# A decoder trunk: the gate of the recurrent layer as a stage of its own with seven products, and the last recurrent block in two token halves

## The chip, the cores and the metric

One core of a Trainium2 chip runs one program. The metric is the device time of one execution in microseconds (us). TensorE does the matrix products, VectorE and ScalarE the elementwise work, GpSimd some elementwise work and the loads that add onto what lies in the buffer, SyncE issues the other loads and stores. Each engine runs its instructions in a fixed order and waits on semaphores.

## The reference

Two layers on 16 learned tokens and 1024 frames, width 1024: a latent attention layer, then a gated linear recurrence. What matters here is the second layer and the end:

```python
def rglru_mixer(h, w_in, conv_w, conv_b, w_rg, b_rg, w_ig, b_ig, lam, w_out):
    proj = h @ w_in
    u, gate = jnp.split(proj, [LRU_WIDTH], axis=-1)
    up = jnp.pad(u, ((0, 0), (CONV_WIDTH - 1, 0), (0, 0)))
    uc = conv_b + up[:, 0:T] * conv_w[0]
    for j in range(1, CONV_WIDTH):
        uc = uc + up[:, j:j + T] * conv_w[j]
    ub = uc.reshape(B, T, LRU_BLOCKS, LRU_BLOCK)
    r = jax.nn.sigmoid(jnp.einsum('btgi,gij->btgj', ub, w_rg).reshape(B, T, LRU_WIDTH) + b_rg)
    i = jax.nn.sigmoid(jnp.einsum('btgi,gij->btgj', ub, w_ig).reshape(B, T, LRU_WIDTH) + b_ig)
    log_a = -LRU_C * r.astype(jnp.float32) * jax.nn.softplus(-lam.astype(jnp.float32))
    a = jnp.exp(log_a)
    mult = jnp.sqrt(-jnp.expm1(2.0 * log_a))
    ...
    b = mult * (i * uc).astype(jnp.float32)
    _, hs = lax.associative_scan(combine, (a, b), axis=1)
    y = hs.astype(h.dtype) * jax.nn.silu(gate)
    return y @ w_out
```

Then come the residual add, a last normalisation, and the output of the 1024 frames. Four recurrent blocks of 256 channels make the 1024 channels.

## The kernel before, in words

Channels lie on the partitions, tokens along the rows. A product of two float32 numbers is made of three matmuls on a high and a low part (`mm3`, lines 86 to 88): high by high, low by high, high by low. `hi_of` (line 80, ScalarE) makes a high part, `lo_of` (line 83, VectorE) the low part as the difference. So each operand of TensorE costs one pass of ScalarE and one of VectorE first.

The normalised input of the second layer is `x2h`, `x2l`, made tile by tile of 128 tokens out of the attention layer's output product (`ao`) and transposes (`xt_b`). Then, by column tile `ct` of 128 channels:

- `b_u(ct)`: the recurrent path, `pu` = 72 matmuls of about 348 columns, copied to `up`, and the convolution `uc` (one ScalarE pass, three VectorE taps), split into `uh` and `ul`.
- `b_gate(ct)`: the gate, `pg` = 2 chunks of 24 matmuls of 512 columns; ScalarE takes the sigmoid, VectorE multiplies with the bank: `Y`.
- `b_rec(blk)`: both gates of the recurrence for two column tiles, `pz` = 72 matmuls, a sigmoid for each bank, then exponential and tanh over 1040 tokens, then the root (each group of functions behind a table load), then VectorE's multiplies and the scan over all tokens (line 813).
- `b_mul(ct)`: `Y` times the scan's result, two halves of 512 tokens, on GpSimd (line 822).

The order by block: gates of the block, recurrence, then `b_u` of the next block. So between a block's convolution and its `pz` stand one or two gate tiles. The last gate (`ct` 7) runs behind the last `pz`.

The output product `b` at the end is cut into quarters: tokens in two halves, channels in two halves, columns in two halves, with seven products of 48 matmuls in place of eight, on sums and differences of quarters (`a11`, `a12`, `a21`, `a22` are quarters of `Y` by channel and token half, `y_split` splits them, `ych`/`ycl` and `y1`, `y7` are the parts). The sums of weights are made by loads that add onto the buffer, issued by GpSimd (`wchain`, `wt`).

The framework orders each engine's instructions from its own estimate of time, so the rows of an engine don't stand in the order of the code. `behind` keeps ScalarE's groups of functions together.

## Time and profile before

| | |
|---|---|
| runs | 915.93, 918.11, 918.83 us; median 918.11 |
| profiled execution | 920.09 us, its span 918.30 us |
| TensorE, VectorE, ScalarE, GpSimd busy | 97%, 64%, 51%, 5% of the span |
| loads and stores | 72.25 MB, 79 GB/s mean |

The span is that of the profiled instructions; the rest of the profiled time lies around it. Busy time of TensorE counts each matmul from start to its modelled end, and neighbours overlap.

### The profile page before, as it was taken

The page shows a single profiled execution, that of the slowest core. Times are in us where ns is not written, and L with a number is a line of the kernel's source. Part 1 is how long each engine was busy: PE and PEld are TensorE (multiplying, and loading weights), DVE is VectorE, ACT ScalarE, POOL GpSimd, SP SyncE. Part 2 cuts the span into 40 slices and gives each one's busy share as a digit, 9 for nine tenths or more (in the row PEclk, how much of TensorE's full clock was granted, in tenths as well). Part 3 has the DMA queues.
Part 4 walks back from the last instruction along what each step waited for, and adds up shares of the span by engine and source line. Part 5 has one row for each costly group of instructions (what it writes and reads, how often), then busy time and mean ns, then how long its engine had stood idle before and what let it go on. Part 6 is the DMA issues. An engine that isn't in the chain of part 4 may idle for free.

```text
...
## 1 busy us (share of the span) xinstructions
...
## 2 busy tenths in 40 slices
...
GB/s 273 47 58 92 64 130 129 83 71 57 16 57 16 17 55 17 16 63 16 17 53 98 144 90 159 87 93 46 46 46 46 47 46 47 92 92 229 137 70 183
DMA packets 71169, 72.25 MB, mean 79 GB/s; under 512 B 15056, under 2 KB 52688, under 8 KB 71104
## 3 DMA queue, kind: packets, MB, share of 16 engines
...
## 4 chain that ended last, share of the span: by engine, by line
PE 92%; ACT 3%; DVE 2%; issue 1%; DMA 1%; SPq 0%; ACTq 0%; DVEq 0%
PE pt L536 4%; PE pu L88 3%; PE ga L86 3%; PE pu L86 3%; PE ga L87 3%; PE ga L88 3%; PE pu L87 3%; PE ao L86 3%; PE ao L88 3%; PE ao L87 3%; PE pg L87 3%; PE pg L88 3%; PE pg L86 3%; PE s L491 2%; PE b L86 2%; PE b L88 2%
## 5 line engine op out<-in xcount | busy, mean ns | idle before, releaser
L509 ACT ACTIVATE p<-s,m 116x116 f32<-116x116 f32 (+4 forms) x80 | 55.3, 693 | 42.9 <-PE pt L536 15.2
L80 ACT ACTIVATE pth<-pt 116x348 fp32r<-116x348 f32 (+5 forms) x152 | 57.5, 396 | 29.4 <-PE pt L536 25.8
L83 DVE TENSOR_TENSOR ptl<-pt,pth 116x348 fp32r<-116x348 f32 (+5 forms) x152 | 64.1, 438 | 10.3 <-ACT pth L80 9.8
L88 PE MATMUL pu<-x2h,l_wu 128*128 128x348 f32 (+1 forms) x192 | 61.5, 321 | 0.4 <-DVE l_wu L83 0.4
L86 PE MATMUL ga<-xth,h_wg 128*128 128x348 f32 (+1 forms) x192 | 61.7, 321 | 0.0
L88 PE MATMUL ga<-xth,l_wg 128*128 128x348 f32 (+1 forms) x192 | 61.7, 321 | 0.0
L87 PE MATMUL pu<-x2l,h_wu 128*128 128x348 f32 (+1 forms) x192 | 61.7, 321 | 0.0
L86 PE MATMUL pu<-x2h,h_wu 128*128 128x348 f32 (+1 forms) x192 | 61.7, 322 | 0.0
L87 PE MATMUL ga<-xtl,h_wg 128*128 128x348 f32 (+1 forms) x192 | 61.6, 321 | 0.0
L501 DVE CUSTOM_DVE_ANT_0 s<-s,maskt 116x116 f32<-116x116 f32 (+8 forms) x72 | 49.4, 686 | 17.8 <-PE s L495 17.7
L536 PE MATMUL pt<-ident,p 116*116 116x116 f32 (+1 forms) x360 | 54.6, 263 | 2.3 <-DVE ptl L83 1.8
L86 PE MATMUL ao<-wah,yh_a 128*128 128x512 f32 x128 | 50.5, 396 | 2.1 <-ACT yh_a L80 1.5
L87 PE MATMUL pg<-x2l,h_wbg 128*128 128x512 f32 x128 | 50.6, 395 | 0.0
L88 PE MATMUL ao<-wah,yl_a 128*128 128x512 f32 x128 | 50.3, 395 | 0.0
L88 PE MATMUL pg<-x2h,l_wbg 128*128 128x512 f32 x128 | 50.3, 393 | 0.0
L86 PE MATMUL pg<-x2h,h_wbg 128*128 128x512 f32 x128 | 50.2, 392 | 0.0
L87 PE MATMUL ao<-wal,yh_a 128*128 128x512 f32 x128 | 49.9, 391 | 0.0
L491 PE MATMUL s<-kh,qh 128*116 128x348 f32 (+7 forms) x120 | 42.1, 351 | 6.7 <-ACT p L509 6.7
L536 PEld LDWEIGHTS pt<-ident,p 116*116 116x116 f32 (+1 forms) x360 | 41.4, 135 | 6.0 <-DVE ptl L83 2.5
L87 PE MATMUL o<-ptl,v 116*128 116x348 f32 (+1 forms) x144 | 45.8, 318 | 0.0
L88 PE MATMUL o<-pth,v 116*128 116x348 f32 (+1 forms) x144 | 44.6, 310 | 0.0
L86 PE MATMUL o<-pth,v 116*128 116x348 f32 (+1 forms) x144 | 43.6, 303 | 0.0
...
## 6 DMA issues: line engine op xcount, KB each, us to landing
wg<-in_a_w_in SPq DMA_DIRECT2D x8, 512.0 KB, 4.0
wa<-in_a_w_out SPq DMA_DIRECT2D x8, 512.0 KB, 3.5
wu<-in_b_w_in SPq DMA_DIRECT2D x8, 512.0 KB, 4.2
wbg<-in_b_w_in SPq DMA_DIRECT2D x8, 512.0 KB, 3.9
hr<-hscr SPq DMA_DIRECT2D x8, 512.0 KB, 6.7
...
x<-in_x SPq DMA_DIRECT2D x7, 512.0 KB, 3.3
wq<-in_b_w_out SPq DMA_DIRECT2D x6, 512.0 KB, 3.5
```

What stands on the lines that cost most here:

```text
L80: nc.scalar.activation(dst, src, AF.Copy)
L83: nc.vector.tensor_tensor(dst, src, bc(hi), ALU.subtract)
L86: nc.tensor.matmul(ps, lh, rh, start=start, stop=False, **kw)
L87: nc.tensor.matmul(ps, lh, rl, start=False, stop=False, **kw)
L88: nc.tensor.matmul(ps, ll, rh, start=False, stop=stop, **kw)
L491: nc.tensor.matmul(ps, a, kth[:, k0:k0 + w], start=True, stop=False)
L501: MKD[h, t] = nc.vector.tensor_tensor_reduce(pv, pv, mk, 1.0, -NEG, ALU.add, ALU.min, m[:, s:s + 1])
L509: MK[h, t] = nc.scalar.activation(dst, pv, AF.Exp, bias=mx, scale=-1.0, accum_out=l[:, s:s + 1])
L536: nc.tensor.transpose(pv[:nk, j], p[:, k0:k0 + nk], ident[:n, :n])
```

## The change: what it does

The gate becomes a stage in front of the recurrence, for all 1024 channels and frames. It is cut into quarters as the output product is: seven products `g1`, `g2`, `g7`, `g6`, `g4`, `g5` and one more onto `g5`'s banks, each 4 banks x 4 k x 3 matmuls of 512 columns, on quarters of `x2` or on sums of them (`x_sum`, `x_split`: `sum_s3` and others, over 2048 elements a partition), with weight quarters and sums of them (`gchain`, `gt1`). The results are added up in `Y`, and ScalarE applies one SiLU at the end.

The recurrence then has `pu` of the next block ahead of `pz` of this one, and the convolution of a block behind the recurrence of the block before. The last block runs its exponentials, roots, multiplies and scan in two token halves, its `pz` in four chunks, and VectorE multiplies `Y`. Residual rows of the first half are loaded earlier.

```diff
-    hs_ = {}
-    after = []
-    us = {0: [b_u(0), b_u(1)]}
-    gates = {0: [0], 1: [1, 2], 2: [3, 4], 3: [5, 6]}
...
-    for blk in range(NBLK):
-        for ct in gates[blk]:
-            b_gate(ct)
-            gated.add(ct)
-        settle()
-        b_rec(blk, us.pop(blk))
-        settle()
-        if blk + 1 < NBLK:
-            us[blk + 1] = [b_u(2 * blk + 2), b_u(2 * blk + 3)]
...
+    def gate_product(banks, w, xx, first=True):
+        xh, xl = xx
+        for m in range(4):
+            for k in range(4):
+                mm3(banks[m], w[0][k // 2][:, k % 2, m * P:(m + 1) * P], w[1][k // 2][:, k % 2, m * P:(m + 1) * P],
+                    xh[:, k], xl[:, k], first and k == 0, k == 3, skip_group_check=True)
+
+    def x_sum(name, tag, a, b):
+
+        s_ = pbg.tile([P, 4, 512], F32, name=f"sum_{name}", tag=tag, bufs=1)
+        bs = [bc(b_) for b_ in b] if isinstance(b, tuple) else [b]
+        nc.vector.tensor_tensor(s_, bc(a[0]), bs[0], ALU.subtract)
+        nc.vector.tensor_tensor(s_, s_, bc(a[1]), ALU.add)
+        for b_ in bs[1:]:
+            nc.vector.tensor_tensor(s_, s_, b_, ALU.subtract)
+        return s_
...
+    x11, x12, x21, x22 = xq(0, 0), xq(1, 0), xq(0, 1), xq(1, 1)
...
+    b1 = four("g1")
+    gate_product(b1, w1, x11)
+    r2 = w_raw("gq21")
+    w_load(r2, 1, 0, w=w_gate)
+    w2 = w_split(r2, pw1, "gq21")
+    for m in range(4):
+        nc.scalar.activation(cq(0, 0, m), b1[m], AF.Copy)
+        nc.scalar.activation(cq(0, 1, m), b1[m], AF.Copy, scale=-1.0)
+    b2 = two_two("g2")
+    gate_product(b2, w2, x12)
+    s3 = x_sum("s3", "suma", x21, x11)
+    w7 = w_split(ra, wpg, "gt3")
+    s2 = x_sum("s2", "sumb", x22, s3)
+    y7 = x_split(s3, "s3")
+    w_load(ra, 0, 0, True, w=w_gate)
+    for m in range(4):
+        nc.vector.tensor_tensor(cq(0, 0, m), b2[m], cq(0, 0, m), ALU.add)
+        silu(0, 0, m)
+    b7 = four("g7")
+    gate_product(b7, w7, y7)
+    w6 = w_split(ra, pw1, "gt2")
+    y6 = x_split(s2, "s2")
+    s1 = x_sum("s1", "suma", x11, s2)
+    s4 = x_sum("s4", "sumc", x12, s2)
...
+    b6 = two_two("g6")
+    gate_product(b6, w6, y6)
...
+        for p0, p1 in parts:
+            ex = []
+            for o in range(2):
+                ct = 2 * blk + o
+                r, a = ri[o][0][:, p0:p1], as_[o][:, p0:p1]
+                ex.append(behind(sig, nc.scalar.activation, a, r, AF.Exp, 0.0, c8[:, ct:ct + 1]))
+                ex.append(behind(sig, nc.scalar.activation, r, r, AF.Tanh, 0.0, c4[:, ct:ct + 1]))
+            sig = []
+            for o in range(2):
+                sig.append(behind(ex, nc.scalar.activation, ri[o][0][:, p0:p1], ri[o][0][:, p0:p1], AF.Sqrt))
...
+    us = conv_pair(0, u_pair(0))
+    for blk in range(LASTB):
+        ups = u_pair(blk + 1)
+        if blk + 1 == LASTB:
+            st_x2.close()
+            st_hr, phr = open_pool("hr", bufs=1)
+            hr = [phr.tile([P, D], F32, name=f"hr{i}") for i in range(4)]
+            for i in range(4):
+                nc.sync.dma_start(hr[i], hscr[NMETA + i * P:NMETA + (i + 1) * P, :])
+            st_b3, pb3 = open_pool("b3", bufs=2)
+        b_rec(blk, us)
+        for o in range(2):
+            b_mul(2 * blk + o)
+        if blk + 1 == LASTB:
+            pool_of = lambda ct: pb3
+        us = conv_pair(blk + 1, ups)
+    HALF = NMETA + 512
+    b_rec(LASTB, us, [(c, 264) for c in (0, 264)] + [(c, 256) for c in (528, 784)], ((0, HALF), (HALF, T)))
...
-    y2 = yc(a12, "a12")
...
+    y2 = y_pair("y2", a12, 1, (("z0", "z0"), ("z1", "z1")))
```

How the instructions stand then, at three places. First VectorE of the changed kernel around `suml_s3`, the low half that the third gate product streams (`l_gt2` are low halves of weights, `Y<-g2` the combinations with the banks of the second product, lines 820 to 823 are `x_sum`); before, none of these rows exists.

```order
L820 TENSOR_TENSOR sum_s3_6966<-x2h_6171 128x2048
L83 TENSOR_TENSOR x2l_6172<-xt_b7_1_6770,x2h_6171 128x4x128
L83 TENSOR_TENSOR l_gt3_1_6975<-gchain_1_6837,h_gt3_1_6974 128x1024
L866 TENSOR_TENSOR Y_1217<-g2_0_6914,Y_1217 128x512
L821 TENSOR_TENSOR sum_s3_6966<-sum_s3_6966,x2l_6172 128x2048
L866 TENSOR_TENSOR Y_1217<-g2_1_6915,Y_1217 128x512
L823 TENSOR_TENSOR sum_s3_6966<-sum_s3_6966,x2l_6172 128x2048
L866 TENSOR_TENSOR Y_1217<-g2_2_6916,Y_1217 128x512
L83 TENSOR_TENSOR l_gt2_0_7048<-gchain_0_6836,h_gt2_0_7047 128x1024
L866 TENSOR_TENSOR Y_1217<-g2_3_6917,Y_1217 128x512
L820 TENSOR_TENSOR sum_s2_6978<-x2h_6171,sum_s3_6966 128x2048
L83 TENSOR_TENSOR l_gt2_1_7052<-gchain_1_6837,h_gt2_1_7051 128x1024
```

The row that follows is `suml_s3`; so it stands behind the combination with the last bank of the second product and a pass of the next sum.

Second, VectorE where the convolution of the last block is made (`uc` the taps, `ul` the low halves that its `pz` needs). Before, from block 2's last scan on:

```order
L813 SCALAR_TENSOR_TENSOR z_0_8009<-a_8062,z_1_8034 128x1040
L768 SCALAR_TENSOR_TENSOR uc_8165<-up_8085,cwt,uc_8165 128x1040 x2
L83 TENSOR_TENSOR l_wq_0_8529<-wq_0_8524,h_wq_0_8528 128x1024
L768 SCALAR_TENSOR_TENSOR uc_8165<-up_8085,cwt,uc_8165 128x1040
L83 TENSOR_TENSOR ul_8171<-uc_8165,uh_8170 128x1040
```

And in the changed kernel (`Y<-Y` is the difference of two quarters of `Y`, `y1l` and `y7h` parts of the output product's operands, `z_1` the multiply of block 2's input gate):

```order
L927 SCALAR_TENSOR_TENSOR uc_8506<-up_8273,cwt,uc_8506 128x1040
L1028 TENSOR_TENSOR Y<-Y 128x4x512
L927 SCALAR_TENSOR_TENSOR uc_8497<-up_8187,cwt,uc_8497 128x1040
L927 SCALAR_TENSOR_TENSOR uc_8506<-up_8273,cwt,uc_8506 128x1040
L970 TENSOR_TENSOR z_1_8400<-z_1_8400,uc_8163 128x1040
L927 SCALAR_TENSOR_TENSOR uc_8497<-up_8187,cwt,uc_8497 128x1040
L927 SCALAR_TENSOR_TENSOR uc_8506<-up_8273,cwt,uc_8506 128x1040
L1037 CAST y7h_8715<-Y 128x1024
L1037 CAST y7h_8719<-Y 128x1024
L788 SCALAR_TENSOR_TENSOR y1l_8712<-Y,y1h_8711 128x1024
L83 TENSOR_TENSOR l_wt_0_8786<-wchain_8702,h_wt_0_8785 128x1024
L970 TENSOR_TENSOR z_1_8450<-z_1_8450,uc_8172 128x1040
```

The row after `y7l` that follows these is `ul` of the first tile; so work for the output product now stands between the taps and `ul`, which it did not.

Third, TensorE ahead of the last block's `pz`. Before, a gate tile ends there:

```order
L86 MATMUL pg_1_8362<-x2h,h_wbg_8331 128x512
L87 MATMUL pg_1_8362<-x2l,h_wbg_8331 128x512
L88 MATMUL pg_1_8362<-x2h,l_wbg_8332 128x512
L86 MATMUL pz_0_0_8399<-uh_8170,h_wri_8394 128x348
L87 MATMUL pz_0_0_8399<-ul_8171,h_wri_8394 128x348
```

Now `pz` of the block before ends there, and six matmuls that need `uh` alone stand first:

```order
L88 MATMUL pz_1_2_8467<-uh_8177,l_wri_8372 128x344
L86 MATMUL pz_0_0_8523<-uh_8502,h_wri_8518 128x264
L86 MATMUL pz_0_1_8531<-uh_8502,h_wri_8518 128x264
L86 MATMUL pz_0_2_8539<-uh_8502,h_wri_8518 128x256
L86 MATMUL pz_0_3_8547<-uh_8502,h_wri_8518 128x256
L86 MATMUL pz_1_0_8556<-uh_8502,h_wri_8518 128x264
L86 MATMUL pz_1_1_8564<-uh_8502,h_wri_8518 128x264
L87 MATMUL pz_0_0_8523<-ul_8503,h_wri_8518 128x264
```

The gate tiles between the two are gone, and the first matmul of the block that needs `ul` is the seventh.

## Rows read from the trace of the kernel before

**Rows 1.** Busy time by stretch: us, then each engine's busy us (instructions), clock, DMA.

```profile
606.50:811.70 205.20, 205.13 (x1143) 190.34 (x1144) 127.84 (x125) 109.58 (x148) 24.23 (x22) 1.00 0.23 60
...
823.00:911.50 88.50, 87.84 (x393) 71.83 (x391) 82.67 (x122) 49.71 (x74) 10.65 (x8) 1.00 0.52 146
```

**Rows 2.** Timeline of TensorE: start, duration, line, tiles, pairs of neighbours.

```profile
640.20 0.39 PE L87 MATMUL pg<-x2l,h_wbg 128*128 128x512 f32 x1
640.43 0.39 PE L88 MATMUL pg<-x2h,l_wbg 128*128 128x512 f32 x1
...
755.83 0.32 PE L87 MATMUL pz<-ul,h_wri 128*128 128x348 f32 x1
755.99 0.32 PE L88 MATMUL pz<-uh,l_wri 128*128 128x348 f32 x1
...
909.35 0.28 PE L86 MATMUL b<-h_wt,ych_a 128*128 128x256 f32 x1
909.47 0.28 PE L87 MATMUL b<-l_wt,ych_a 128*128 128x256 f32 x1
```

**Rows 3.** Timeline of VectorE: a scan, two taps, and four neighbours of other sizes.

```profile
779.32 2.32 DVE L813 TENSOR_TENSOR_SCAN z<-a,z 128x1040 f32<-128x1040 f32 x1
...
788.26 2.61 DVE L768 SCALAR_TENSOR_TENSOR uc<-up,cwt,uc 128x1040 f32<-128x1040 f32 x2
...
849.07 0.68 DVE L960 TENSOR_TENSOR hr<-b,hr 128x512 f32<-128x512 f32 x1
849.67 2.28 DVE L1020 TENSOR_TENSOR Y<-Y 128x2048 f32<-128x2048 f32 x1
851.87 1.21 DVE L83 TENSOR_TENSOR l_wq<-wq,h_wq 128x1024 fp32r<-128x1024 f32 x1
853.01 0.68 DVE L962 TENSOR_TENSOR hr<-hr,b 128x512 f32<-128x512 f32 x1
```

**Rows 4.** Timeline of ScalarE: a table load, exponentials, tanh, and two of 512.

```profile
767.21 1.28 ACT L308 ACT_TABLE_LOAD   x1
768.50 2.22 ACT L308 ACTIVATE a<-z,c 128x1040 f32<-128x1040 f32 x2
770.63 2.20 ACT L308 ACTIVATE z<-z,c 128x1040 f32<-128x1040 f32 x2
...
807.70 1.06 ACT L308 ACTIVATE Y<-pg 128x512 f32<-128x512 f32 x2
```

**Rows 5.** Timelines of TensorE and VectorE: where `pu` begins to run, the last `x2l`.

```profile
606.57 0.43 PE L88 MATMUL pu<-x2h,l_wu 128*128 128x348 f32 x1 [0.42 <-DVE l_wu L83]
...
615.82 0.69 DVE L83 TENSOR_TENSOR x2l<-xt_b,x2h 128x512 fp32r<-128x512 f32 x1 [0.23 <-ACT x2h L80]
```

**Rows 6.** DMA issues: the loads that add, KB each, median us to landing.

```profile
wchain<-in_b_w_out POOLq DMA_DIRECT2D x6, 512.0 KB, 6.1
```

**Rows 7.** Timelines of GpSimd and VectorE: multiplies on GpSimd, alone and beside VectorE.

```profile
687.74 1.30 POOL L822 TENSOR_TENSOR Y<-Y,z 128x512 f32<-128x512 f32 x1 [0.46 <-DVE Y L837]
...
781.78 4.37 POOL L822 TENSOR_TENSOR Y<-Y,z 128x512 f32<-128x512 f32 x2 [32.04 <-DVE z L813]
...
784.93 3.41 DVE L813 TENSOR_TENSOR_SCAN z<-a,z 128x1040 f32<-128x1040 f32 x1
```

**Rows 8.** Busy time by stretch, as rows 1, where the granted clock fell.

```profile
506.00:507.00 1.00, 0.97 (x6) 0.89 (x6) 0.57 (x2) 0.66 (x2) 0.00 (x0) 0.70 0.70 246
507.00:508.00 1.00, 1.00 (x6) 1.00 (x5) 0.55 (x2) 0.35 (x2) 0.00 (x0) 0.50 0.05 16
...
509.00:510.00 1.00, 1.00 (x6) 1.00 (x5) 0.00 (x0) 0.00 (x0) 0.00 (x0) 0.59 0.00 0
510.00:511.00 1.00, 1.00 (x8) 1.00 (x7) 0.00 (x0) 0.00 (x0) 0.00 (x0) 1.00 0.91 299
```

**Rows 9.** Timeline of TensorE there: the wait before it, and two neighbours in it.

```profile
504.10 0.93 PE L536 MATMUL pt<-ident,p 116*116 116x116 f32 x5 [1.22 <-DVE ptl L83]
...
508.24 0.49 PE L87 MATMUL o<-ptl,v 116*128 116x344 f32 x1
508.52 0.49 PE L88 MATMUL o<-pth,v 116*128 116x344 f32 x1
```

More of the change, by code (lines that the diff above doesn't have):

```diff
@@ new lines, in x_sum, with x_split @@
+    def x_sum(name, tag, a, b):
[6 more added lines that the diff above has]
+        return s_
+    def x_split(s_, name):
+        xh = pbg.tile([P, 4, 512], F32R, name=f"sumh_{name}", tag="sumh", bufs=2)
+        xl = pbg.tile([P, 4, 512], F32R, name=f"suml_{name}", tag="suml", bufs=2)
+        hi_of(xh, s_)
+        lo_of(xl, s_, xh)
+        return xh, xl
@@ new lines, in four, with two_two, silu @@
+    def four(name):
+        return [ps_m(f"{name}_{m}") for m in range(4)]
+    def two_two(name):
+        return [(ps_m if m < 2 else ps_t)(f"{name}_{m}") for m in range(4)]
+    def silu(tq, nq, m):
+        v = cq(tq, nq, m)
+        nc.scalar.activation(v, v, AF.Silu)
+    x11, x12, x21, x22 = xq(0, 0), xq(1, 0), xq(0, 1), xq(1, 1)
+    r1 = w_raw("gq11")
+    w_load(r1, 0, 0, w=w_gate)
+    w1 = w_split(r1, wpg, "gq11")
+    ra = w_raw("gchain")
+    w_load(ra, 0, 1, w=w_gate)
+    w_load(ra, 1, 1, True, w=w_gate)
@@ new lines, in trunk @@
+    w4 = w_split(ra, wpg, "gt4")
+    r5 = w_raw("gt1")
+    w_load(r5, 0, 0, w=w_gate)
+    w_load(r5, 0, 1, True, w=w_gate)
+    for m in range(4):
+        nc.vector.tensor_tensor(cq(1, 1, m), b6[m], cq(1, 1, m), ALU.add)
+        nc.vector.tensor_tensor(cq(0, 1, m), b6[m], cq(0, 1, m), ALU.add)
+    b4 = four("g4")
+    gate_product(b4, w4, x22)
+    w5 = w_split(r5, pw1, "gt1")
+    y5 = x_split(s1, "s1")
+    for m in range(4):
+        nc.vector.tensor_tensor(cq(1, 0, m), b4[m], cq(1, 1, m), ALU.subtract)
+        silu(1, 0, m)
@@ new lines, in trunk @@
+    b5 = two_two("g5")
+    gate_product(b5, w5, y5)
+    r3 = w_raw("gq22")
+    w_load(r3, 1, 1, w=w_gate)
+    w3 = w_split(r3, wpg, "gq22")
+    y3 = x_split(s4, "s4")
+    for m in range(4):
+        nc.vector.tensor_tensor(cq(1, 1, m), b5[m], cq(1, 1, m), ALU.add)
+        silu(1, 1, m)
+    gate_product(b5, w3, y3, False)
+    for m in range(4):
+        nc.vector.tensor_tensor(cq(0, 1, m), b5[m], cq(0, 1, m), ALU.add)
+        silu(0, 1, m)
+    st_bg.close()
+    st_bw, pbw = open_pool("bw", bufs=2, side="right")
@@ new lines, in trunk, with b_u @@
+    pool_of = lambda ct: pbw
+    def b_u(ct):
+        raw = load_wcols(b_w_in, ct * P, KT, P, f"wu{ct}")
+        wh, wl = split_page(raw, [P, KT, P], f"wu{ct}")
+        up = pbw.tile([P, CW - 1 + T], F32, name=f"up{ct}", tag="up", bufs=2)
+        nc.gpsimd.memset(up[:, :CW - 1], 0.0)
+        for c, (c0, cw) in enumerate(CH):
+            ps = ps_m(f"pu{ct}_{c}")[:, :cw]
+            for k in range(KT):
+                mm3(ps, wh[:, k], wl[:, k], x2h[:, k, c0:c0 + cw], x2l[:, k, c0:c0 + cw], k == 0, k == KT - 1)
+            nc.scalar.activation(up[:, CW - 1 + c0:CW - 1 + c0 + cw], ps, AF.Copy)
+        return up
@@ new lines, in b_conv @@
+    def b_conv(ct, up):
+        uc = pool_of(ct).tile([P, T], F32, name=f"uc{ct}", tag="uc", bufs=2)
+        nc.scalar.activation(uc, up[:, :T], AF.Identity, bias=bcol[:, 0, ct:ct + 1], scale=cwt[:, 0, ct:ct + 1])
+        for j in range(1, CW):
+            nc.vector.scalar_tensor_tensor(uc, up[:, j:j + T], cwt[:, j, ct:ct + 1], uc, ALU.mult, ALU.add)
+        uh = pool_of(ct).tile([P, T], F32R, name=f"uh{ct}", tag="uh", bufs=2)
+        ul = pool_of(ct).tile([P, T], F32R, name=f"ul{ct}", tag="ul", bufs=2)
+        hi_of(uh, uc)
+        lo_of(ul, uc, uh)
+        return uc, uh, ul
```

185 lines of the change are left out of this document (80 added, 105 removed).

## The prediction

> **What bounds the kernel now.** First the page: TensorE is busy 97% of the span. Busy time can hide waits, so I read the windows of the part that changes: from 606.50 to 811.70 us TensorE is busy 205.13 of 205.20 us, and from 823.00 to 911.50 it is busy 87.84 of 88.50 [rows 1]. After 606.5 us nothing but the number of columns streamed sets the end: a matmul taken out is worth its time, and a wait put in costs its whole length. The same rows show who could become the next bound: in the last window VectorE is busy 82.67 of 88.50 us, so the output products run with 6 us of slack on VectorE.
>
> Matmuls overlap, so the 0.39 us of one is not its price. The distance between two starts is: 0.23 us for 512 columns, 0.16 for 348, 0.12 for 256 [rows 2].
>
> **What the change removes.** The gate before is 8 column tiles x 2 chunks x 24 matmuls = 384 of 512 columns. Afterwards it is 7 products of 48, so 336. 48 x 0.232 = **11.1 us less** of TensorE. The last block's `pz` goes from 72 matmuls of about 348 columns (72 x 0.158 = 11.4) to 96 of 264 or 256 (96 x 0.123, between the last two of these distances, = 11.8): **0.4 more**.
>
> **What it takes away as cover.** Before, between the convolution of a block and its `pz`, TensorE had one or two gate tiles (11.1 us each) to run; that is how the long VectorE chains cost nothing. Now the gates stand ahead. I walk the four places where TensorE meets VectorE, with the steps, start to start [rows 3, 4]: VectorE 0.6 us for 512 elements, 1.15 for 1024 or 1040, 2.2 for 2048, 2.3 for a scan, 1.2 to 1.3 for a convolution tap; ScalarE 0.53 for 512, 1.06 for 1040, 1.28 for a table load. Estimates for half widths are half-way rows (528 elements: 0.57 on ScalarE, 0.6 on VectorE).
>
> **Place 1, third product of the gate stage (`g7`).** It needs `sum_s3` = x21 - x11, so the whole of `x2`. Before, TensorE began its run at 606.57, and the last low half of `x2` came at 615.82 [rows 5]. Afterwards 8 gate matmuls (1.9 us) run earlier, so I put the run at 608.1; 40 matmuls of the first product (9.3), 8 transposes (0.8) and the second product (11.1) bring TensorE to 629.3. ScalarE has to copy the first product out twice before it converts the last x2 tile: three page splits until 616.0, six copies x 0.53, one conversion 0.6, then 0.6 on VectorE: 620.4. From there VectorE's row of work up to `suml_s3` is fixed by its order: one conversion 0.6, three passes of s3 6.6, three page splits 3.45, four combinations with `g2` 2.4, one pass of s2 2.2, `suml_s3` 2.2: 17.45 us, so 637.9. TensorE can do 4 matmuls (0.9) meanwhile: **7.7 us** of wait. Lower bound without any backlog: the last `g2` combination can't start before the last matmul of `g2`, and 0.6 + 2.2 + 1.15 + 2.2 stand from there to the end of `suml_s3`; less 0.9: 5.2. Upper bound 10, if the accumulating load of the weights, 6.1 us to landing [rows 6], also comes late. The later products have 2 us or more in hand by the same walk. The bytes of the stage more than double (nine quarter loads of 1 MB against eight tiles of 0.5), beside a DMA share of 0.23 [rows 1]: hidden.
>
> **Place 2, `pz` of blocks 1 and 2.** From the end of one `pz` to the next there are now only 144 `pu` matmuls (22.8 us) and 18 of `pz` that need no `ul` of the second tile (2.8): 25.6. The chain: on ScalarE a page split, last sigmoid, load, 2 exponentials, 2 tanh, `uh`, an `up`, load, 2 roots and a `uc`: 12.9 us; on VectorE from there five steps of 1.15 (three multiplies, a split and `ul`), two taps and both scans: 12.9 more; and the two GpSimd multiplies by the scan's result. GpSimd and VectorE hold each other up: two such multiplies took 4.37 us beside VectorE and a single one 1.30, and the scan under them 3.41 [rows 7] against 2.32 [rows 3]; twice 1.1 us. Sum 28.0, so **2.4 us** for block 1; in block 2 `ul` stands ahead of the second scan: **0.6**. Bounds 0 and 6 together.
>
> **Place 3, `pz` of the last block.** Its `pu` is done one block earlier, and only block 2's `pz` (11.4 us) stands between. Count from S, the start of that `pz`. VectorE ends the scans of block 1 at S + 5.7 (the chain of place 2). Then, in its order, one page split, six taps, the difference of the Y quarters, two multiplies, two casts, `y1l`, a split, `y7l` and `ul6`: 1.15 + 7.2 + 2.2 + 2.3 + 1.2 + 4.6 = 18.65, and 1.6 for GpSimd's multiplies, which the Y difference must also wait for: S + 25.9. TensorE is out of work at S + 12.0, and has 6 matmuls (0.7) with `uh` alone. **13.2 us** of wait, the largest term. Lower bound: `uh6` stands behind the sigmoids of block 2, a table load and two exponentials on ScalarE: S + 18.4 at the earliest, `ul6` 1.2 later, so 7.5. Upper bound 16.
>
> **Place 4, the products after the recurrence.** The first two need channels 0 to 511 alone and give 22.3 us of cover. Count from Z, the end of the last `pz`. The first exponentials and roots of the half take ScalarE to Z + 6.8. VectorE then has, up to `ycl_s2`, 26 steps of 0.6, 11 of 1.15 or a half scan, and 4 of 2.2: 37.1 us, without a gap, so Z + 44.4 with the hand-overs. TensorE needs it after three products and 16 matmuls, at Z + 37.1: **7.3**, and 0.5 for the two GpSimd multiplies that now fall here: **7.8**. This is the slack of the last window used up: it had 88 us of TensorE work with 82.67 of VectorE [rows 1], now 78 with about as much of VectorE. Bounds 3 and 10.
>
> ScalarE has two more table loads in the last block. A load takes 1.28 us, and the exponential starts right behind it, 768.50 after 767.21 [rows 4]. The Trainium skill, "ScalarE: Activation LUTs", section "What ACT_TABLE_LOAD costs", adds a drain of about 1.38 us to each switch; by it places 3 and 4 would each wait some 1.4 to 2.8 us longer, by the row nothing. The trace does not show such a gap, so the sum leaves it out.
>
> **The clock.** After a wait of 1.22 us [rows 9] and thin work the granted clock of TensorE fell to 0.50 (1.2 GHz of 2.4) for some 3.3 us [rows 8], in which matmuls of 344 columns stood 0.29 us apart [rows 9] and not 0.16: 11 matmuls x 0.13 = 1.4 us. Places 1, 3 and 4 have longer waits: 3 x 1.4 = **4.2**. Lower bound 0, upper 6.
>
> **Sum:** - 11.1 + 0.4 + 7.7 + 2.4 + 0.6 + 13.2 + 7.8 + 4.2 = + 25.2 us. The profiled execution took 920.09 us (span 918.30, 1.79 around it), 1.98 above the median of the runs, 918.11. So 945.3 in a like profile, and **943 us** as a median.
>
> **Rivals.**
> - *Only the hard bounds hold* (VectorE's backlog is smaller than I count, because it catches up in gaps that I don't see): 5.2 + 0 + 7.5 + 3, and 2.8 for the clock: - 10.7 + 18.5 = + 7.8, 926 us. For it: VectorE is idle for more than a third of 606.5 to 811.7, 77 of 205 us [rows 1]. Against it: at the four places its rows stand one behind another.
> - *Covered waits, faster*: the convolution of the last block is done while `pz` of block 2 runs, and TensorE's queue never empties: - 10.7, 907 us. It would need `ul6` by S + 12; it decides as soon as all the waits and the clock together are below 10.7. For it: the run before hides chains of 40 us without a wait. Against: place 3 alone can't be below 7.5, place 1 not below 5.2, and these two make 12.7; the chance that I leave it is for an error in these bounds.
> - *Each wait at its upper bound* (GpSimd and the loads also in VectorE's way): 10 + 6 + 16 + 10 + 6 - 10.7 = + 37, 955 us.
> - *The gate stage does not do seven products*: the order shows 336 matmuls; no chance given.
>
> **Chances.** My sum 0.62, the hard bounds 0.2, upper bounds 0.12, covered 0.06. 0.3% (2.8 us) is about what a measurement here can tell. Range 925 to 955: it takes in the sum and the hard bounds, and leaves out the covered case and part of the upper one. Faster 0.06, same 0.03, slower 0.91.
>
> **What would show it.** In the changed profile: waits of `g7` on VectorE's `suml` of 5 to 10 us; waits of the last block's `pz` on `uh` and `ul` of 8 to 16 us together, right after block 2's `pz`; waits of the `b` products on `ych` and `ycl` of 3 to 10 us; slices at a granted clock of 0.5 behind each. TensorE's count down by 48 matmuls of 512 columns. The prediction is wrong if TensorE shows less than 11 us of waits after 606 us, or if the large wait stands at a place that I have not named.

## The result, and the profile after

The changed kernel takes 957.24 us as a median (955.32 to 958.96), the kernel before beside it 918.47: ratio 1.0417 (95% interval 1.0372 to 1.0462). Timed once more, with the experiments, it took 958.17, ratio 1.0425 (1.0400 to 1.0450). So it is 39 us slower, where 25 had been forecast (943, range 925 to 955): the direction was right, the size 14 us short.

The page of the changed kernel, busy time of each engine and the granted clock in 40 slices:

```profile
span 957.2 us, 13763 instructions
PE 897.0 (94%) x5267; PEld 821.4 (86%) x5267; DVE 628.8 (66%) x1253; ACT 490.0 (51%) x972; POOL 54.2 (6%) x52
PEclk9999999999999999999997999989999999879899
```

Busy time misleads here. TensorE has 48 matmuls of 512 columns fewer in its program, and yet is busy for 897.0 us, 5.2 more than before, because five slices of the clock's row stand below 9: its matmuls were slower there. The windows that answer to [rows 1] show the waits that came:

```profile
606.50:811.70 205.20, 195.42 (x1056) 177.54 (x1056) 128.57 (x117) 103.03 (x136) 19.08 (x19) 0.98 0.31 79
...
860.00:949.80 89.80, 82.63 (x352) 65.90 (x350) 83.53 (x126) 48.92 (x78) 10.00 (x8) 0.94 0.40 112
```

TensorE now idles for 9.8 of the 205.2 us, and for 7.2 in the output products. What it waits for is listed by the waits of TensorE (us in total, times, longest):

```profile
PE pz L86 <- ACT uh L80: 9.2, 3, 6.6
PE g L86 <- ACT sumh_s L80: 6.8, 1, 6.8
...
PE pz L87 <- DVE ul L83: 6.6, 3, 4.0
PE b L86 <- ACT ych_s L787: 5.4, 2, 2.8
PE pt L536 <- DVE ptl L83: 5.4, 4, 3.7
...
PE b L88 <- DVE y2l L788: 1.6, 1, 1.6
```

Five of the six are the four places of the prediction. The sixth, `pt` on `ptl`, lies near 500 us in the attention layer. It was 1.8 us in the same list of the kernel before, and nothing was forecast there.

The rest is in the clock. The windows of TensorE's work behind each wait, chosen so that they hold little else, in the order of time (attention, place 1, place 2, place 3, place 4):

```profile
507.50:514.90 7.40, 7.18 (x29) 6.48 (x30) 3.25 (x14) 1.89 (x5) 0.00 (x0) 0.53 0.27 94
640.70:642.70 2.00, 2.00 (x4) 1.15 (x4) 1.96 (x1) 0.98 (x2) 0.90 (x1) 0.50 0.49 51
643.10:648.00 4.90, 4.90 (x13) 3.85 (x14) 4.87 (x3) 1.91 (x1) 0.00 (x0) 0.55 0.51 92
...
823.90:829.00 5.10, 5.10 (x19) 5.10 (x20) 5.10 (x3) 4.51 (x8) 2.84 (x2) 0.55 0.36 128
...
846.90:853.00 6.10, 6.10 (x30) 6.10 (x31) 6.05 (x7) 4.26 (x7) 0.00 (x0) 0.55 0.32 57
...
904.30:911.00 6.70, 6.70 (x17) 5.25 (x18) 6.70 (x9) 1.11 (x4) 0.00 (x0) 0.55 0.42 152
```

Work done at a granted clock of 0.50 (1.2 GHz of 2.4) takes nearly twice as long, so a stretch costs about its busy time x (1 - clock): at place 1, 2.00 x 0.50 + 4.90 x 0.45 = 3.2 us. Summed in the same way over windows of 1 us from 600 us on, the loss is 13.6 us (3.3, 2.9, 3.6 and 3.8 at places 1 to 4); near 500 us it is 4.0, against 1.7 before. In place 1 the matmuls show it directly:

```profile
644.11 0.63 PE L86 MATMUL g<-sumh_s,h_gt 128*128 128x512 f32 x1
644.53 0.63 PE L87 MATMUL g<-suml_s,h_gt 128*128 128x512 f32 x1
```

They stand 0.42 us apart and not 0.23 [rows 2]; that is 1.8 times as far and not twice, so the losses given here are some tenth too high.

**The sum.** Waits after 590 us 30.6 (added up over TensorE's timeline, 0.5 before): + 30.1. Waits near 500 us: 5.4 - 1.8 = + 3.6. Clock: + 13.6 from 600 us on, + 2.3 near 500 us, and - 1.7 for half clock at 49 to 53 us, which only the profile of the kernel before has. Matmuls: - 10.7. Together + 37.2; the spans differ by 957.2 - 918.3 = 38.9. The rest of 1.7 us and the tenth by which the clock's loss is too high are not accounted for one by one. Each of some eleven new waits also breaks the row of overlapping matmuls, so that the last one ahead of it counts 0.39 us and not 0.23 [rows 2]: 1.8 us, by estimate.

### The profile page after: what moved, and what is told of

Its sections match the earlier page's. It is cut to its first block, busy times and chain, and to the rows that moved or that the text cites. A ratio compares the mean times of both kernels' runs of the same rounds, so it can differ in the third digit from the quotient of the medians.

```text
span 957.2 us, 13763 instructions
## 1 busy us (share of the span) xinstructions
PE 897.0 (94%) x5267; PEld 821.4 (86%) x5267; DVE 628.8 (66%) x1253; ACT 490.0 (51%) x972; POOL 54.2 (6%) x52
## 4 chain that ended last, share of the span: by engine, by line
PE 80%; DVE 6%; ACT 6%; DMA 5%; issue 2%; SPq 1%; ACTq 0%; DVEq 0%; POOLq 0%
PE pt L536 3%; PE ga L86 3%; PE ga L87 3%; PE ga L88 3%; PE ao L86 3%; PE ao L88 3%; PE ao L87 3%; PE pu L86 2%; PE pu L88 2%; PE pu L87 2%; PE s L491 2%; PE g L87 2%; PE o L88 2%; PE o L87 2%; PE o L86 2%; PE s L492 2%
## 5 line engine op out<-in xcount | busy, mean ns | idle before, releaser
L509 ACT ACTIVATE p<-s,m 116x116 f32<-116x116 f32 (+4 forms) x80 | 55.4, 693 | 42.9 <-PE pt L536 15.2
L87 PE MATMUL pz<-ul,h_wri 128*128 128x348 f32 (+3 forms) x104 | 35.1, 338 | 6.6 <-DVE ul L83 6.6
L86 PE MATMUL pz<-uh,h_wri 128*128 128x348 f32 (+3 forms) x104 | 32.7, 337 | 9.2 <-ACT uh L80 9.2
L493 PE MATMUL s<-kh,ql 128*116 128x348 f32 (+7 forms) x120 | 39.4, 328 | 0.0
```

The source lines that it names most:

```text
L86: nc.tensor.matmul(ps, lh, rh, start=start, stop=False, **kw)
L87: nc.tensor.matmul(ps, lh, rl, start=False, stop=False, **kw)
L493: nc.tensor.matmul(ps, b_, kth[:, k0:k0 + w], start=False, stop=False)
L509: MK[h, t] = nc.scalar.activation(dst, pv, AF.Exp, bias=mx, scale=-1.0, accum_out=l[:, s:s + 1])
```

## The experiments

Times are medians beside runs of the kernel before on the same chip. The column "to the changed kernel" is (ratio - 1.0425) x 918. Idle time of TensorE from 590 us on and the clock's loss from 600 us on are of the profiled run, worked out as above; the first row shows how far two profiles of one kernel differ (30.6 and 13.6 in the first).

| run | us | ratio to before | to the changed kernel | idle | clock |
|---|---|---|---|---|---|
| after_again | 958.17 | 1.0425 (1.0400 to 1.0450) | 0 | 31.5 | 12.7 |
| late_tables | 949.78 | 1.0342 (1.0320 to 1.0364) | - 7.6 | 29.8 | 11.5 |
| fill_waits | 952.68 | 1.0381 (1.0359 to 1.0402) | - 4.0 | 16.6 | 4.9 |
| conv_ahead | 957.74 | 1.0441 (1.0421 to 1.0462) | + 1.5 | 33.0 | 9.3 |
| plain_gates | 957.45 | 1.0429 (1.0412 to 1.0447) | + 0.4 | 27.5 | 3.9 |
| sum_first | 952.97 | 1.0369 (1.0343 to 1.0395) | - 5.1 | 30.0 | 6.1 |
| y_behind | 960.50 | 1.0448 (1.0424 to 1.0472) | + 2.1 | 32.7 | 12.7 |
| no_halves | 953.86 | 1.0376 (1.0351 to 1.0402) | - 4.5 | 32.1 | 9.9 |
| before_bc_right | 925.11 | 1.0069 (1.0053 to 1.0085) | | 0.4 | 0.0 |
| mul_vector | 953.52 | 1.0379 (1.0362 to 1.0395) | - 4.2 | 28.9 | 10.4 |
| three_undone | 947.17 | 1.0303 (1.0285 to 1.0320) | - 11.2 | 29.0 | 10.5 |
| plain_front | 952.85 | 1.0368 (1.0351 to 1.0386) | - 5.2 | 26.4 | 4.9 |
| tiles_back | 946.88 | 1.0307 (1.0286 to 1.0329) | - 10.8 | 20.9 | 6.1 |
| before_gates_first | 963.37 | 1.0483 (1.0461 to 1.0506) | | 31.4 | 12.1 |
| tiles_back_sigmoid | 946.06 | 1.0289 (1.0271 to 1.0307) | - 12.5 | 19.1 | 6.9 |

> The changed kernel itself, unchanged, to stand beside the next runs on the same chip: 955 to 959 us, ratio to the kernel before 1.040 to 1.044. No theory is tested by it.

It did.

### The fifth place: the small tables in the attention's end

In the changed kernel's trace TensorE stands still from 501.1 to 504.9 us, and ScalarE's timeline shows why:

```profile
501.71 0.21 ACT L737 ACTIVATE t<-bcol 128x8 f32<-128x8 f32 x1 [4.47 <-DMA bcol<-in_b_lam]
501.93 1.28 ACT L738 ACT_TABLE_LOAD   x1
503.23 0.21 ACT L738 ACTIVATE t<-t 128x8 f32<-128x8 f32 x1
503.34 0.60 ACT L80 ACTIVATE pth<-pt 116x348 fp32r<-116x348 f32 x2
```

ScalarE waited 4.47 us for the recurrence's parameters, loaded a table, and only then made `pth`, for which the attention was waiting. These instructions stood 120 us later before. What moved them is a line of the change on which I had put no price: the pool of these tables lies on the other side of the memory, `open_pool("bc", bufs=1, side="right")`, presumably where space comes free earlier, and so their loads and steps ran earlier. Two runs, one on each kernel. The first moves the computation:

```diff
-    lam = bcol[:, 3]
-    nc.scalar.activation(t1, lam, AF.Abs)
...
-        silu(0, 1, m)
+        sl = silu(0, 1, m)
     st_bg.close()
+    lam = bcol[:, 3]
+    behind([sl], nc.scalar.activation, t1, lam, AF.Abs)
...
```

> The changed kernel, with the recurrence's small tables (absolute value, sigmoid with its table load, 15 small VectorE steps) issued behind the last SiLU of the gate stage, and not in the attention's end. Theory (a fifth place that the prediction missed): ScalarE stood 4.47 us for the table's load at 497 to 502 us, TensorE idled 3.6 us more than before, and its matmuls after it ran at half clock for 2.3 us worth more; so 957.2 falls by 5 to 6.5 us, to about 951, and TensorE's idle time before 590 us is that of the kernel before. Rival 1 (the tables cost the same wherever they stand, now at the gate stage's end): no change, a new wait of some 4 us at pu. Rival 2 (attention's end waits for another reason): no change, same idle time there.

The time fell by 7.6 us (949.78), a little more than forecast. The idle time before 590 us is that of the kernel before, the loss by clock near 500 us 1.7 us as before. In the profile the gate stage begins 6.2 us earlier (596.0 us against 602.2). No new wait stands at `pu`. Both rivals fall. The second run moves only the pool, in the kernel before:

```diff
-    st_bc, pbc = open_pool("bc", bufs=1)
+    st_bc, pbc = open_pool("bc", bufs=1, side="right")
...
-    st_bc.close()
...
     st_w1.close()
+    st_bc.close()
```

> The kernel before, with one edit of the change alone: the pool of the recurrence's small tables on the right side, closed at the end. TensorE's order is the same as before. Theory (the side lets these tables run in the attention's end, and ScalarE waits there for their load): 5 to 7.5 us slower than the kernel before, ratio 1.005 to 1.008, with waits on ptl of 5 to 6 us in all near 500 us and a longer half clock there. Rival (the tables only hurt together with the gate stage): ratio 0.998 to 1.002.

925.11 us, ratio 1.0069: 6.3 us slower. The timeline of its ScalarE, and the waits of its TensorE:

```profile
501.92 0.21 ACT L737 ACTIVATE t<-bcol 128x8 f32<-128x8 f32 x1 [4.21 <-DMA bcol<-in_b_lam]
```

```profile
PE pt L536 <- DVE ptl L83: 5.8, 4, 3.5
```

So about a sixth of the change's loss has nothing to do with gates or halves.

### The clock: the price of a wait

```diff
+    def fill(ps, rhs, n):
+        for _ in range(n):
+            nc.tensor.matmul(ps, nul, rhs, start=True, stop=True, skip_group_check=True)
...
+    for m in range(4):
+        fill(b7[m], x2h[:, m, NMETA:NMETA + 512], 6)
     gate_product(b7, w7, y7)
...
                     ps = ps_m(f"pz{ct}_{gt}_{c}")[:, :cw]
+                    if blk == LASTB and not o and not gt and not c:
+                        fill(ps[:, :256], wh[:, 0, 0], 84)
```

`nul` is a tile of zeros.

> The changed kernel, with TensorE kept streaming in the two longest waits: 24 matmuls of 512 columns with a zero operand ahead of g7 (24 x 0.232 = 5.6 of 7.1 us) and 84 of 256 columns ahead of the last block's pz (some 9 to 10 of 10.5 us), into banks that the real product overwrites. The waits on VectorE and ScalarE stay as long as they were. Theory (the half clock is the price of the idle time, 3.3 us after place 1 and 3.6 after place 3): granted clock stays at 1.00 there and the time falls by 6 to 7 us, to about 950.5, with 108 matmuls more. Rival 1 (the slow matmuls have another cause): no change. Rival 2 (the added matmuls get in the way of the real ones): 1 to 4 us slower.

The kernel with 108 matmuls more is faster, by less than forecast: 952.68 us, 4.0 us by the ratios and 6.4 by the profiled spans. The windows of the filled wait, of the real work behind it, and of the work behind the wait at place 3:

```profile
633.00:640.00 7.00, 6.72 (x29) 5.14 (x28) 6.75 (x7) 3.57 (x4) 1.34 (x2) 1.00 0.66 114
...
642.00:648.00 6.00, 5.86 (x25) 4.76 (x26) 5.96 (x4) 1.92 (x1) 0.00 (x0) 1.00 0.53 85
843.80:849.00 5.20, 5.11 (x29) 5.11 (x30) 5.20 (x6) 3.19 (x6) 0.00 (x0) 0.67 0.40 72
```

At place 1 the clock stays at 1.00 and the loss of 3.3 us is gone: the real work behind the wait runs at full speed. At place 3 the filling ended before `ul` came, TensorE waited another 3.2 us, and half the loss stayed (1.7 of 3.6 us). At place 1 the first rival falls: seven profiles with the wait there lost 1.9 to 3.3 us behind it, this one nothing, so the half clock is the price of the wait ahead of it. Place 3 agrees, less sharply: 2.3 to 4.1 us in other profiles of the same waits. Places 2 and 4, which weren't filled, also lost 3.5 us less than in the profile of the changed kernel. That is not the edit's doing, and it is why I don't read the 6.4 us as the fills' worth. Place 2 in particular lost 1.5 to 2.9 us in five profiles, and nothing in six others with the same waits. The Trainium skill, "Perfetto Trace Analysis", section "Matmul Optimizations", says that TensorE's power follows its use and that matmuls should run back to back; this run agrees, 3.3 us against 0 at place 1.

### Place 1: not VectorE's row of work

The prediction had `suml_s3` late by VectorE's order. The trace of the changed kernel names `sumh_s3` of ScalarE, and the timelines say why, VectorE's with the last pass of the sum, then ScalarE's:

```profile
631.38 2.28 DVE L823 TENSOR_TENSOR sum_s<-sum_s,x2l 128x2048 f32<-128x2048 f32 x1
```

```profile
637.78 1.06 ACT L80 ACTIVATE h_gt<-gchain 128x1024 fp32r<-128x1024 f32 x1 [4.31 <-DMA gchain<-in_b_w_in]
638.75 1.89 ACT L80 ACTIVATE sumh_s<-sum_s 128x2048 fp32r<-128x2048 f32 x1
```

The sum was ready at 633.7. Its high half stood in ScalarE's queue behind a weight split of the next product, which waited 4.31 us for an accumulating load.

```diff
-    s2 = x_sum("s2", "sumb", x22, s3)
     y7 = x_split(s3, "s3")
+    both = [last["hi"], last["lo"]]; s2 = behind(both, x_sum, "s2", "sumb", x22, s3)
...
-    w6 = w_split(ra, pw1, "gt2")
+    w6 = behind(both, w_split, ra, pw1, "gt2")
```

> The changed kernel, with the split of the third x sum (sumh_s3, suml_s3) put ahead of the next weight sum's split on ScalarE and VectorE, and the next x sum behind it. Theory (place 1 is not VectorE's row of work, as predicted, but ScalarE's queue: sum_s3 was ready at 633.7, and sumh_s3 stood behind a weight split that waited 4.31 us for an accumulating load): g7 starts at about 635.6 and not 640.7; the waits there fall from 7.1 to 2 to 3.5 us and the half clock behind them goes in part; the time falls by 4 to 7 us. Rival (VectorE's row of work sets suml_s3, the prediction's reason): the wait moves from sumh_s3 to suml_s3 and the time falls by less than 2.5 us.

952.97 us, 5.1 less. ScalarE then makes the half when the sum is there:

```profile
633.55 1.91 ACT L80 ACTIVATE sumh_s<-sum_s 128x2048 fp32r<-128x2048 f32 x1 [1.56 <-DVE sum_s L823]
635.36 1.04 ACT L80 ACTIVATE h_gt<-gchain 128x1024 fp32r<-128x1024 f32 x1
```

The waits there fall from 7.1 to 2.9 us (1.73 and 1.19), and 1.8 us turn up at the next products. The rival falls: what was in VectorE's row was not what came last. In the profiles the gate stage, from its first matmul to its last, is 3.1 us shorter than in the changed kernel (94.5 us against 97.6; 95.5 to 97.9 in the seven profiles that leave it as it was). About as much lies behind place 3, where the edit does nothing and the clock lost less; so not all of the gain is place 1's.

The same queue takes part at place 4, which the prediction laid on VectorE alone. The sum behind the second wait on `ych_s` was ready at 899.66 us, and ScalarE began its high half at 902.28, behind a weight split that waited for an accumulating load:

```profile
897.38 2.28 DVE L1136 TENSOR_TENSOR Y<-Y 128x2048 f32<-128x2048 f32 x1
```

```profile
900.10 1.06 ACT L80 ACTIVATE h_wt<-wt 128x1024 fp32r<-128x1024 f32 x1 [1.30 <-DMA wt<-in_b_w_out]
...
902.28 1.90 ACT L787 ACTIVATE ych_s<-Y 128x2048 fp32r<-128x2048 f32 x1
```

TensorE waited 2.66 us there. No run changes this order.

The other half of the question is what the seven products are worth, when the sums must be waited for:

```diff
-    x11, x12, x21, x22 = xq(0, 0), xq(1, 0), xq(0, 1), xq(1, 1)
...
+    for ct in range(KT):
+        b_gate(ct)
```

> The changed kernel, with the gate stage kept in front but made of eight plain column tiles (384 matmuls of 512 columns, no sums of x quarters). Theory (the saved product is paid back by the wait for the sums): 48 x 0.232 = 11.1 us more of TensorE, 7.1 us less of waiting at place 1 and 3.3 us less of half clock: +0.7 us, 956 to 959, no change. Rival 1 (the wait moves on to the next place): 965 or more. Rival 2 (the sums and their loads disturb more than place 1): 950 or less.

957.45 us, no change. 11.1 us more of matmuls cost next to nothing, because the wait at place 1 (7.1 us) and the half clock behind it (3.3) went with the sums: in the profiles the stage takes 99.1 us with eight tiles, and 95.5 to 97.9 with seven products.

### Place 3: order, chain or cover

The prediction gave 13.2 us here, for VectorE's row of work with the pieces of the output product ahead of `ul`. First VectorE's and ScalarE's order (block 2's exponentials behind `uh7`, the pieces behind `ul7`):

```diff
+            pool_of = lambda ct: pb3 if ct >= 2 * LASTB else pbw
+            nxt = conv_pair(blk + 1, ups)
+            hold, low = [last['hi']], last['lo']
+        b_rec(blk, us, hold=hold)
...
-                ex.append(behind(sig, nc.scalar.activation, a, r, AF.Exp, 0.0, c8[:, ct:ct + 1]))
+                ex.append(behind([*sig, *hold], nc.scalar.activation, a, r, AF.Exp, 0.0, c8[:, ct:ct + 1]))
...
+    behind([low], nc.vector.tensor_tensor, a21, a21, a11, ALU.subtract)
...
+    y1 = behind([low], y_pair, "y1", a11, -1, (("up", "up"), ("uh", "ul")))
```

> The changed kernel, with the last block's convolution put ahead of what need not come first: the difference of the Y quarters, y1 and y7 behind ul7 on VectorE, and block 2's exponentials behind uh7 on ScalarE. Theory (place 3 is VectorE's and ScalarE's order, not their amount of work): the two waits there fall from 10.5 to about 4 us, and part of the 3.6 us of half clock goes; 957.2 falls by 7 to 10 us, to 947 to 950. Rival (VectorE's backlog is what counts, so what place 3 loses place 4 gets back): waits of the b products grow by 5 us or more, and the time falls by less than 3 us.

957.74 us, no gain. The waits of TensorE in this run:

```profile
PE pz L86 <- ACT uh L80: 7.5, 3, 5.0
PE pz L86 <- ACT z L308: 6.9, 1, 6.9
...
PE b L86 <- ACT y2h L787: 6.6, 1, 6.6
...
PE pz L87 <- DVE ul L83: 3.7, 3, 1.7
```

The waits on `uh` and `ul` at place 3 did fall, from 10.5 to 5.5 us. A new one of 6.9 us took their place inside `pz`: its banks were free only when ScalarE had read them, behind the exponentials that were held back. And `y2h` came 6.6 us late. With VectorE's order alone (the diff is against conv_ahead):

```diff
-            hold, low = [last['hi']], last['lo']
-        b_rec(blk, us, hold=hold)
+            low = last['lo']
+        b_rec(blk, us)
```

> The changed kernel, with only VectorE's order changed at place 3: the difference of the Y quarters and the splits y1, y7 behind ul7 (block 2's exponentials stay where they are). Theory (order at place 3): the wait on ul6 falls from 4.0 to below 1 us, no bank waits for a late sigmoid, the time falls by 3 to 5 us. Rival (backlog: block 2's scans are now later, so place 4 pays): the wait on ul6 falls as well, but the waits of the b products grow from 7.0 us by as much, and the time stays within 2 us.

960.50 us. Place 3 waits 11.5 us in three pieces (4.9 and 3.6 on `uh`, 3.0 for a bank), and place 4:

```profile
PE b L86 <- ACT y2h L787: 10.0, 1, 10.0
```

Neither theory holds. `y_behind` went as its rival says, with the b products' waits 3.0 us longer; in `conv_ahead` they grew by 1.0 us only, and the wait moved to the banks of `pz`. In both a step that comes earlier at place 3 makes another come later. Next the multiplies by the scan's result, from GpSimd to VectorE:

```diff
-            nc.gpsimd.tensor_tensor(yv, yv, r[:, c0:c0 + 512], ALU.mult)
+            nc.vector.tensor_tensor(yv, yv, r[:, c0:c0 + 512], ALU.mult)
```

> The changed kernel, with the multiplies of Y by the scan's result of blocks 0 to 2 on VectorE and not on GpSimd. Theory (GpSimd and VectorE hold each other up: two taps took 4.57 us beside such a multiply and 2.50 alone, so VectorE loses about 4.3 us a block and would pay 4 x 0.6 = 2.4): waits at places 2 and 3 shrink by 1.5 to 3 us in all, time 1 to 4 us lower. Rival (VectorE is the late one there, so more work on it costs its length): 2 to 5 us slower.

953.52 us, 4.2 less. VectorE has four steps a block more and is done with the taps earlier. The first two taps of the last block's convolution in the changed kernel, and here:

```profile
827.12 4.57 DVE L927 SCALAR_TENSOR_TENSOR uc<-up,cwt,uc 128x1040 f32<-128x1040 f32 x2
```

```profile
825.24 2.50 DVE L927 SCALAR_TENSOR_TENSOR uc<-up,cwt,uc 128x1040 f32<-128x1040 f32 x2
```

The taps are what the theory said; the waits, by their sum, are not. Place 2 fell from 5.3 to 2.3 us, but place 3 grew from 10.5 to 13.3. What the edit brought is seen by the start of the recurrence's first `pz` and the end of the last block's wait on `ul`:

| run | first `pz`, us | `ul` there, us | between | clock's loss at place 2 |
|---|---|---|---|---|
| changed kernel | 745.60 | 846.86 | 101.3 | 2.9 |
| late_tables | 738.72 | 839.90 | 101.2 | 2.6 |
| sum_first | 742.38 | 843.57 | 101.2 | 0 |
| no_halves | 743.26 | 844.38 | 101.1 | 0 |
| plain_front | 740.98 | 842.27 | 101.3 | 0 |
| mul_vector | 746.08 | 842.92 | 96.8 | 0 |

The chain over the other engines has one length in the first five, whether TensorE lost 2.9 us at place 2 or nothing: there the half clock costs nothing, since the next waits are shorter by about as much. Without the multiplies on GpSimd the chain is 4.4 us shorter, and the time fell by 4.2. The Trainium skill, "Perfetto Trace Analysis", section "Optimizing Scalar/DVE Operations", says that GpSimd and VectorE share a port, so that moving work between them might not help; 4.57 against 2.50 us agrees with the port, and here the move did help.

Then the cover. In the kernel before one line takes it away, with all else as it was:

```diff
-    gates = {0: [0], 1: [1, 2], 2: [3, 4], 3: [5, 6]}
+    gates = {0: [0, 1, 2, 3, 4, 5, 6], 1: [], 2: [], 3: []}
```

> The kernel before with one line changed: the gate tiles 0 to 6 all ahead of block 0's recurrence, none between the blocks; the last tile stays behind the last pz, and pu still stands behind the pz of the block before. Theory (cover): ahead of each pz of blocks 1 to 3 TensorE waits for a whole convolution of the second tile, some 7 to 9 us, and runs at half clock after it: 24 to 36 us slower, 942 to 955. Rival (the chains are hidden by pu and need no gate tile): below 925.

963.37 us, ratio 1.0483: 45 us slower, 8 us above the range. Nearly all of the waiting is one line of the waits:

```profile
PE pz L86 <- ACT uh L80: 30.8, 6, 9.1
```

That is 9 to 12 us a block, in two waits each, where 7 to 9 had been forecast. 30.8 us of waits and 12.1 of clock make 42.9 of the 43.3 us by which the spans differ. The same number of matmuls, the same elementwise work. Then the changed order with three other parts put back: the edits of plain_gates and late_tables and that of no_halves (below) together:

> The changed kernel, with eight plain gate tiles in the stage in front, tables behind that stage, no token halves: so the gate's TensorE work is that of the kernel before, and only its place (in front and not between the blocks) and the order pu, pz, convolution are the change's. Theory (cover is what was lost: the same tiles in front cover nothing): waits of pz and b of 20 to 25 us with 6 to 9 us of half clock, 945 to 950 us, ratio 1.030 to 1.035. Rival (the seven products, the halves and the tables make most of the 39 us): below 935 us.

952.85 us, a little above the range. The waits:

```profile
PE pz L86 <- ACT uh L80: 9.8, 3, 7.2
PE pz L87 <- DVE ul L83: 8.1, 3, 4.9
...
PE b L86 <- ACT y2h L771: 5.7, 1, 5.7
```

With 1.9 us on `y2l` they make 25.5, and 4.9 us of clock stand beside them: 30.4 of the 31.4 us by which its span (949.7) is longer than before. That is the price of the gate's place together with the new order, with `pu` ahead of `pz` as a partial cover. (Singly the three edits made - 7.6, - 4.5 and + 0.4 us, together - 5.2, so their worths don't add up.) Two tiles back in their old places:

```diff
-    for ct in range(KT):
+    for ct in range(KT - 2):
         sl = b_gate(ct)
...
+    b_gate(KT - 2)
     b_rec(LASTB, us)
+    b_gate(KT - 1)
```

(The input `x2` then lives longer, so the last block has no buffers of its own and shares two with block 2.)

> The kernel plain_front with two of its eight gate tiles taken out of the stage in front: tile 6 stands between pz of block 2 and pz of block 3, tile 7 behind the last pz. The work of every engine is the same. Theory (place 3 and place 4 are lost cover, whatever the order of VectorE's rows): the waits of 12.1 us on uh and ul and 7.6 us on y2 fall to below 2 us each, with the half clock behind them, and the time falls by 20 to 26 us from 952.9, to 927 to 933. Rival (VectorE's backlog is the bound, so the waits turn up at the next product): 943 or more.

946.88 us: 6.0 less than plain_front, not 20 to 26. Place 4 has no wait left on parts of `Y`, so there the theory holds: tile 7 behind the last `pz` pays for it. Place 3 waits 12.4 us as before, part of it for a new reason:

```profile
PE pz L86 <- ACT Y L838: 5.9, 2, 4.5
```

Those are banks whose SiLU stood behind table loads of its own. Without these loads:

```diff
-            sl = nc.scalar.activation(Y[:, ct, c0:c0 + 512], ps, AF.Silu)
+                sl = behind(marks, nc.scalar.activation, yv, ps, AF.Sigmoid)
+                nc.vector.tensor_tensor(yv, ps, yv, ALU.mult)
```

> The kernel tiles_back, with the two tiles that were put back activated as in the kernel before: a sigmoid in the same group as the recurrence's sigmoids and a multiply on VectorE, and not a SiLU with two table loads of its own between block 2's roots. (In tiles_back place 4 had no wait on the parts of Y any more, but place 3 still waited 12.4 us, 5.9 of it for banks whose SiLU stood behind table loads.) Theory (place 3 is lost cover too, spoilt there by ScalarE's queue): the waits at place 3 fall from 12.4 to 3 to 6 us, and the time from 946.9 to 936 to 941. Rival (place 3 is the length of the chain over ScalarE and VectorE itself, one tile of 11.1 us is not enough cover): waits of 9 us or more there, 944 or more.

946.06 us, and 11.2 us of waits at place 3 (5.5 for banks, 3.3 on `uh`, 2.4 on `ul`). The rival's numbers. One tile of 11.1 us did not cover it. In this run the second tile's convolution shared VectorE with block 2's multiplies and the gate's own steps, and ScalarE waited for its taps:

```profile
830.77 1.07 ACT L80 ACTIVATE uh<-uc 128x1040 fp32r<-128x1040 f32 x1 [6.37 <-DVE uc L884]
```

The shared buffers are a second difference, so these two runs don't tell the length of the chain from them. What the smallest cure of place 3 is stays open; shown is that a change of VectorE's order isn't it, and that all the cover of the kernel before is enough.

### The halves, and three edits together

```diff
-    b_rec(LASTB, us, [(c, 264) for c in (0, 264)] + [(c, 256) for c in (528, 784)], ((0, HALF), (HALF, T)))
+    b_rec(LASTB, us)
+    for o in range(2):
...
+            nc.vector.tensor_tensor(yv, yv, r[:, NMETA + c * 512:NMETA + c * 512 + 512], ALU.mult)
```

> The changed kernel, with the last recurrent block over all tokens at once, its pz in three chunks of 348 and 344, and VectorE multiplying Y afterwards. Theory (the halves bring y2 forward, the chain of a whole block behind the last pz is some 5 us longer): waits of the b products grow from 7.0 to 10 to 14 us, 3 to 8 us slower than the changed kernel. Rival 1 (VectorE's backlog alone counts, the halves only cut the same work in two): within 2 us. Rival 2 (the halves cost more in short steps and table loads than they bring): 2 us or more faster.

953.86 us, 4.5 less, so by the time rival 2. The trace doesn't bear it out: from the end of the wait on `ul` at place 3 to the last matmul the profiled run takes 102.8 us (844.4 to 947.2), the changed kernel 102.9 (846.9 to 949.8). Waits for parts of `Y` are 7.6 us against 7.0. Behind place 3 the halves neither bring nor cost anything. The gain of the profile lies ahead of it, and ahead of the first `pz` (743.26 us against 745.60): place 1 waits 0.9 us less and loses 1.3 less to the clock. The half clock at place 2 isn't there either, but the table above shows that this is worth nothing. Place 1, which the edit doesn't touch, waits 6.2 to 7.5 us in the seven profiles that leave it as it was, so this is no sign of the halves; where the 4.5 us of the medians come from stays open.

Then the edits of late_tables, sum_first and no_halves together:

> The changed kernel, with the three edits that each brought something put together: tables behind the gate stage, the split of the third x sum first, no token halves. Theory (the three are at different places and add up: 7, 5 and 4 us): ratio to the kernel before 1.0425 - 0.0175 = 1.025, 940 to 943 us. Rival (what TensorE gains early it waits for at place 3, since the chain there is VectorE's): waits of the last block's pz above 13 us, 945 to 950 us.

947.17 us: 11.2 less and not 17, in the rival's range, but its waits at place 3 are 12.1 us and not above 13. They are as long in no_halves, which like this run loses nothing to the clock at place 2, so they are no sign of the rival. If the 4.5 us of no_halves aren't the halves' (above), the other two make 12.7 us, of which 11.2 came. That they then add up is argued, not shown.

## Why the prediction was wrong in size, point by point

- **What bounds the kernel** (TensorE sets the end, a wait costs its whole length): right where no further wait follows, and not enough there: a wait costs more than its length. In the recurrence the chain over the other engines sets the time, and half clock of TensorE costs nothing.
- **48 matmuls fewer, - 11.1; `pz` in four chunks, + 0.4**: as counted. plain_gates shows that all but 1 to 4 us of the 11.1 are paid back at place 1.
- **Place 1, 7.7 us**: 7.1 measured. That the size came out is luck: TensorE was out of work at 633.9 us and not 630.2, `suml_s3` came at 643.1 and not 637.9. The reason was wrong: ScalarE's queue behind an accumulating load, which the prediction had as its upper bound, and not VectorE's row (sum_first).
- **Place 2, 2.4 + 0.6**: 2.1 and 3.2 measured; the second was too small. That GpSimd and VectorE hold each other up is shown by mul_vector, where 2.3 of the 5.3 us are left.
- **Place 3, 13.2**: 10.5. Right place, both waits on `uh` and `ul` as named. Both ends came later than counted: `ul6` at S + 30.1 and not S + 25.9, TensorE out of work at S + 17.9 and not S + 12.0 (S is 816.76 us), so the nearness is in part luck. The order of VectorE, from which it was worked out, was not what a cure needs (conv_ahead, y_behind). The lower bound of 7.5 is 6.9 by its own terms (19.6 - 12.0 - 0.7).
- **Place 4, 7.8**: 7.0, at `y2l` and twice at `ych_s`, the last time by ScalarE's queue and not VectorE's work; cover takes it away (tiles_back).
- **The waits together**: 31.7 forecast, 29.9 at the same places (the five lines above and 0.3 on `suml_s3`).
- **The clock, "3 x 1.4 = 4.2", upper bound 6**: this is the step that failed. That half clock follows a wait was right, its size was not. The one stretch of [rows 8], behind a wait of 1.22 us, was taken as the price of every wait (by the measure used here it cost 1.7 us). At the three places named, 1, 3 and 4, it measured 3.3, 3.6 and 3.8 us, 10.7 together; 2.9 more stood at place 2, where they took the place of waits, and 2.3 near 500 us. With 13.6 in place of 4.2 the sum would have been + 34.6, some 953 us.
- **The fifth place**: a term that the prediction put at nothing without a reason, since it had no line for the pool's side. Waits of 3.6 us and 2.3 of clock near 500 us (late_tables, before_bc_right). With the clock's 9.4 above the forecast that is 15.3 us; the waits, forecast 1.8 us too high, leave 13.5 of the missing 13.7 (38.9 against 25.2), as far as the sum above closes. Without this place the time is 949.78 us (late_tables), inside the range.
- **Rivals**: "covered waits" needed `ul6` by S + 12; the last block's `pz` ran out of work at 834.7 and `ul6` came at 846.8. The upper bounds gave 955 us, the nearest, but by longer waits, which did not come.
- **The drain behind a table load**: none. The sigmoid behind the load of 501.93 + 1.28 starts at 503.23 in the changed kernel.
